# FFN 2 of a streaming-encoder layer: the third and fourth feature tile as a pair job, its operands made during the second halves of the first four units

## The chip, the cores and the metric

One core of one Trainium2 chip. The metric is the device time in microseconds of one execution of the whole layer. Times inside the layer are given on the clock of the profile, from the first instruction of the span.

## What is computed

The reference is one layer of a hybrid encoder on a sequence of 512 tokens with 1024 channels in float32. Only its last part matters here, behind the projection `w_o` of the mixed branches:

```python
h = h + rms_norm(merged @ w_o[l], mix_post_g[l])
f = swiglu(rms_norm(h, ffn2_pre_g[l]), ffn2_w1[l], ffn2_w3[l], ffn2_w2[l])
h = h + 0.5 * rms_norm(f, ffn2_post_g[l])
# swiglu(x, w1, w3, w2) = (silu(x @ w1) * (x @ w3)) @ w2, hidden width D_FF = 2816
```

The first FFN, the input projection, the recurrent branch and the attention come before it and are not touched.

## The kernel before

Every matrix product is made of three products of split operands: a float32 tile is split into a high part (ACT's copy to a shorter format) and a low part (DVE's difference), and the PE adds high x high, low x high and high x low into one PSUM bank. `split2` is one such split: one ACT and one DVE instruction. Weights of an FFN come as feature tiles of 128 columns ("w1b 0" is the first of W1 of FFN 2, "w3b 0" of W3); there are 22 of each.

FFN 2 makes the hidden features in two ways. A *classic unit* takes one feature tile: 8 slices of k times 3 products of 128x512 (`mm_feat`, L201 to L203). A *pair job* takes two feature tiles of the same matrix and the four quarters of x^T (two halves of the channels by two halves of the tokens), and makes the 2x2 block product with seven block products instead of eight (`Pairs.run`); each block product is `mm_s`: 4 slices of k times 3 products of 128x256 (L452 to L454). For that, sums of weight blocks are wanted (`S12`, `S34`, made by `prep(m, 0)` with four additions, on POOL unless told otherwise, L497 to L500, and split by `prep(m, 2)` and `prep(m, 3)`), the first weight tile split (`prep(m, 1)`) and the last block (`prep(m, 4)`), and sums of the quarters of x^T (`sums`: the tiles T, from the four unsplit quarters `xf`; split by `to_slots` and `to_uT` into t1 to t4). In `run`, the first product goes into the bank `bu` and ACT copies it to q1 (L529); the second goes into `bx` and is copied to q5; the third adds on to `bu`. Job m belongs to W1 (even m) or W3 (odd m).

Every engine runs its instructions in the order in which the program issues them. Work that is to run beside later products is put off by `later(n, ...)` and issued at the n-th following `point()`; the queues of loads are SP's, `order` gives the loads' order, and `dma_to`, `split_to` and `get` issue loads and splits up to a given place of it. All large tiles share 42 slots of 4 KB for each partition; a tile takes its slot at its first write, and slots are handed out in the order in which they were freed. A load therefore waits on SP until the last reader of the slot's former tile is done.

`tok_gemm` makes a product with tokens as rows (here merged @ W_o) in four row tiles, with a norm after each (`norms`: L264, L276 and others on DVE, L275 and L283 on ACT), and then transposes the normed rows to x^T (`transpose_mm` on PE, `transpose_out` and `transpose_xf` on ACT and DVE; uT holds x^T split, `xf` unsplit). While the last row tiles are normed, the PE makes the *first halves* (tokens 0 to 255) of the first four classic units, w1b 0, w3b 0, w1b 1, w3b 1; the last transposes stand ahead of the fourth of these. The *second halves* (tokens 256 to 511) follow, then the function returns. Before the change four more classic units come then (w1b 2, w3b 2, w1b 3, w3b 3, NC2 = 4), and the sums of x^T, their splits and the operands of job 0 are issued by `later` during these; then 18 pair jobs.

Of the kernel before, what the change touches and what calls it, by code (L numbers as in the profile page):

```python
# [13 lines left out]
ALU = mybir.AluOpType  # L14
# [4 lines left out]
KT = D // P  # L19
# [32 lines left out]
def hybrid_layer(ctx: ExitStack, tc: tile.TileContext, a: dict, out: bass.AP):  # L52
    nc = tc.nc
    act, dve, pool, pe, sp = nc.scalar, nc.vector, nc.gpsimd, nc.tensor, nc.sync
# [120 lines left out]
    def later(n, fn, rank=1):  # L175
        uid[0] += 1
        due.append((now[0] + n, rank, uid[0], fn))
# [128 lines left out]
    def transpose_xf(banks, t, xf):  # L306
        for half, ps in enumerate(banks):
            v = ps.rearrange("p (k c) -> p k c", k=4)
            act.activation(xf[half, t // 2][:, :, (t % 2) * P : (t % 2 + 1) * P], v, AF.Copy)


    def tok_gemm(nm, xs, n, R, gpost_name, scale, gpre_name, first, x_to=None, xf=None, spill=False):

        F = n - R
        acc = {}
        w = {}

        def accs(t):  # L320
            if t not in acc:
                acc[t] = [bank("acc"), bank("acc")]
            return acc[t]

        pre = min(2, F)
        x_to = x_to or (lambda k: None)
        for k in range(pre):
            x_to(k + 1)
            w[k] = get(nm, k, ahead=pre - k + 1)
        if pre:  # L330
            for tt in ((0, 1), (2, 3)):
                for k in range(pre):
                    for t in tt:
                        mm_tok(accs(t), xs[k], t, w[k], k == 0, False)
                        if t % 2:
                            point()
        for k in range(pre, F):
            x_to(k + 2)
            w[k] = get(nm, k, ahead=2 + (R - 2) * (k + 1) // F)
            for t in range(NT):  # L340
                mm_tok(accs(t), xs[k], t, w[k], k == 0, False)
                if t % 2:
                    point()
        point(True)
        for k in range(F, n):
            x_to(k + 1)
            w[k] = get(nm, k, ahead=max(0, n - 1 - k), rawahead=2)
        gpost = bcast(gpost_name)
        gpre = bcast(gpre_name) if gpre_name else None
        us, trs = {}, {}  # L350
        split_to(st["get"] + len(first))
        dma_to(st["split"] + 2)
        for t in range(NT):
            for ns in ((0,), (1,)):
                for k in range(F, n):
                    mm_tok(accs(t), xs[k], t, w[k], k == 0, k == n - 1, ns)
            if not gpre_name:
                o = slot([P, D], name="o")

                def store(nn, c, t=t, o=o):  # L360
                    sp.dma_start(out=out[t * P : (t + 1) * P, c], in_=o[:, c])

                post_norm(acc[t], t, gpost, scale, o, store)
                continue
            if t == NT - 1:
                break
            if t >= 1:
                trs[t - 1] = transpose_mm(us[t - 1])
            if t == NT - 2:

                transpose_out(trs[t - 1], t - 1)
            us[t] = norms(acc[t], t, gpost, scale, gpre, spill)
            if t == NT - 2 and xf:
                transpose_xf(trs[t - 1], t - 1, xf)
            elif t == 1:
                transpose_out(trs[t - 1], t - 1, xf)
        if not gpre_name:
            return
        t = NT - 1
        ws, bs = [], []  # L380
        for i, key in enumerate(first):
            ws.append(get(*key, ahead=len(first) - 1 - i, rawahead=2))
            bs.append(bank("f"))
            if i == len(first) - 1:
                trs[t] = transpose_mm(us[t])
                transpose_out(trs[t], t)
                if xf:
                    transpose_xf(trs[t - 1], t - 1, xf)
                    transpose_xf(trs[t], t, xf)
            mm_feat(bs[i], ws[i], 0, 256)  # L390
            if i == 0:
                trs[t - 1] = transpose_mm(us[t - 1])
                us[t] = norms(acc[t], t, gpost, scale, gpre, spill)
                transpose_out(trs[t - 1], t - 1)
        get_ahead()
        for w_, b in zip(ws, bs):
            mm_feat(b, w_, 256, 512)
        return bs
# [58 lines left out]
    class Pairs:  # L457
# [13 lines left out]
        def prep(self, m, i, eng=None):  # L471
            if m >= len(self.jobs) or (m, i) in self.ready:
                return
            self.ready.add((m, i))
            k = self.k0 + 2 * m
            if i == 0:
                if k not in loaded or k + 1 not in loaded:
                    self.raws(m)
                s12, s34 = slot([P, 2 * QH], name="S12"), slot([P, 2 * QH], name="S34")
                self.w[m] = {"r": (raws.pop(k), raws.pop(k + 1)), "s": (s12, s34)}  # L480
            W = self.w[m]
            (ra, rb), (s12, s34) = W["r"], W["s"]
            a11, a12, a21, a22 = ra[:, :QH], ra[:, QH:], rb[:, :QH], rb[:, QH:]

            def both(src, w=2 * QH):
                hi = slot([P, w], F32R, name="whi")
                lo = slot([P, w], F32R, name="wlo")
                split2(hi, lo, src)
                return hi, lo

            def halves(p, a, b):
                W[a] = p[0][:, :QH], p[1][:, :QH]
                W[b] = p[0][:, QH:], p[1][:, QH:]

            if i == 0:
                e = eng or pool
                e.tensor_tensor(out=s12[:, :QH], in0=a21, in1=a22, op=ALU.add)  # L497
                e.tensor_tensor(out=s12[:, QH:], in0=s12[:, :QH], in1=a11, op=ALU.subtract)
                e.tensor_tensor(out=s34[:, QH:], in0=a12, in1=s12[:, QH:], op=ALU.subtract)
                e.tensor_tensor(out=s34[:, :QH], in0=a11, in1=a21, op=ALU.subtract)  # L500
            elif i == 1:
                halves(both(ra), "a11", "a12")
            elif i == 2:
                halves(both(s12), "s1", "s2")
            elif i == 3:
                halves(both(s34), "s3", "s4")
            elif i == 4:
                t = slot([P, 2, QH], F32R, name="w22")
                split2(t[:, 0, :], t[:, 1, :], a22)
                W["a22"] = t[:, 0, :], t[:, 1, :]  # L510
                del W["r"], W["s"]
# [109 lines left out]
    hid, X1 = Hidden(), {}  # L621
# [96 lines left out]
    def uview(hh, th):  # L718

        return lambda e, k: uT[:, e, 4 * hh + k, th * 256 : th * 256 + 256]  # L720
# [1 line left out]
    def pair_view(p):  # L722
        return lambda e, k: p[e][:, k, :]

    def sums(xf):

        t = [slot([P, 4, 256], name="T") for _ in range(4)]
        pool.tensor_tensor(out=t[2], in0=xf[1, 1], in1=xf[0, 1], op=ALU.subtract)
        dve.tensor_tensor(out=t[0], in0=xf[0, 1], in1=xf[0, 0], op=ALU.subtract)
        dve.tensor_tensor(out=t[1], in0=xf[1, 1], in1=t[0], op=ALU.subtract)  # L730
        dve.tensor_tensor(out=t[3], in0=xf[1, 0], in1=t[1], op=ALU.subtract)
        return t
# [21 lines left out]
    for k in range(KT):  # L754
        later(2 + k // 2, lambda k=k: norm_x(k))
    later(6, lambda: xts.clear())
    later(6, lambda: tn.extend(sums(xn)))
    later(7, lambda: X1.update(b11=to_slots(xn[0, 0])))
    later(9, lambda: X1.update(t1=to_slots(tn[0])))
    later(11, lambda: X1.update(t2=to_slots(tn[1])))  # L760
# [342 lines left out]
    mg = []  # L1103
# [16 lines left out]
    del xh, xl, OH, OL, KS, QS, BT  # L1120
    h_load([h_scr[t] for t in range(NT)])
    xf = {(hh, th): slot([P, 4, 256], name="xf") for hh in range(2) for th in range(2)}
    bs = tok_gemm("wo", mg, KT, RO, "mix_post_g", 1.0, "ffn2_pre_g", [("w1b", 0), ("w3b", 0), ("w1b", 1), ("w3b", 1)], xf=xf)


    hid = Hidden()
    X2, tn = {"b11": uview(0, 0), "b21": uview(1, 0), "b22": uview(1, 1)}, []
    later(1, lambda: hid.f.append(silu_mul(bs[0], bs[1])))
    later(2, lambda: hid.f.append(silu_mul(bs[2], bs[3])))
    later(1, lambda: tn.extend(sums(xf)))  # L1130
    later(2, lambda: xf.clear())
    for i in range(3):
        later(2 + i, lambda i=i: X2.update({f"t{i + 1}": to_slots(tn[i])}))
    pairs_b = Pairs("w1b", "w3b", NC2, X2, hid)
    end = 2 * 2 * (NC2 - 2)
    for i, at_ in enumerate((end - 7, end - 4, end - 3, end - 2, end - 1)):
        later(at_, lambda i=i: pairs_b.prep(0, i))
    later(end, lambda: pairs_b.prep(1, 0))
    swiglu_units("w1b", "w3b", 2, NC2, hid)
    point(True)  # L1140
    X2["t4"] = to_uT(tn[3], 0, 1)
    tn.clear()
    pairs_b.run(w2_ahead)
    X2 = pairs_b = None
    tok_gemm("w2b", hid, FT, RF, "ffn2_post_g", 0.5, None, [], hid.to)
# [13 lines left out]
RO = 6  # L1159

NC1 = 6
NC2 = 4


# [52 lines left out]
```

## Time and profile before

| | |
|---|---|
| median of 3 runs | 1138.76 us (1138.6 to 1138.85) |
| the profiled execution, its own time | 1138.66 us |
| its span, first to last instruction | 1136.9 us |
| PE, DVE, ACT, POOL busy | 1128.2, 778.7, 582.2, 340.7 us |
| first halves begin on PE | 781.94 us |
| second halves begin | 795.44 us |
| classic units of tiles 2 and 3 begin | 806.96 us |
| pair jobs begin | 828.75 us |

A row of the order of time reads: start, duration, engine, line, operation, what is written and read, shapes (and how many were merged); in brackets the idle time of the engine before it and what ended it. Matmuls overlap in the pipeline: the distance between their starts is what one costs, not the duration shown. A row of waits reads: who, for what, us in total, times, longest.

### The profile page before, as it was taken

To read this page: it belongs to the slowest core of one execution; us is meant where nothing else is said; L and a number is where in the kernel's file an instruction comes from. 1 tells how busy PE (TensorE), PEld (TensorE's weight loads), DVE (VectorE), ACT (ScalarE), POOL (GpSimd) and SP (SyncE) were. 2 spreads that over 40 slices of the span, in tenths; PEclk is the share of its full clock that TensorE was granted. 3 is DMA by queue.
4 is the path that set the end of the run, shared out by engine and by line. 5 is a ranking of instruction groups with operands and counts; after the bars stand their busy time and mean duration, and the time that the engine had idled before them with its cause. 6 is when DMAs were issued, how large, how long until landed. Compare 5 with 4: busy or idle time off the path is not lost.

```text
span 1136.9 us, 17091 instructions
## 1 busy us (share of the span) xinstructions
PE 1128.2 (99%) x6691; PEld 1001.0 (88%) x6691; DVE 778.7 (68%) x1183; ACT 582.2 (51%) x1036; POOL 340.7 (30%) x257
## 2 busy tenths in 40 slices
PE   9999999999999999999999999999999999999997
PEld 7889999988889977888888888889899999998886
DVE  5997889885436745684778854667968678985313
ACT  7445555564325369944656652356445555574211
POOL 0148677500001000001555640000655567700000
PEclk9999999999999999999999999999999999999999
DMA  9943223264314311334122333532123332254101
GB/s 343 158 132 112 96 92 111 82 216 157 104 55 146 132 56 56 90 96 130 56 85 83 93 109 98 176 118 93 39 93 112 112 103 84 93 193 176 40 19 55
DMA packets 36800, 124.93 MB, mean 110 GB/s; under 512 B 4400, under 2 KB 5936, under 8 KB 36720
## 3 DMA queue, kind: packets, MB, share of 16 engines
q1 hardware_dynamic: 34128, 115.15, 30.3%
q0 software_dynamic: 2448, 8.43, 3.8%
q8 instruction: 52, 0.85, 0.3%
q10 hardware_dynamic: 144, 0.26, 0.1%
q14 instruction: 28, 0.23, 0.1%
HBM read 116.50 MB, written 7.33 MB: 109 GB/s over the span
## 4 chain that ended last, share of the span: by engine, by line
PE 97%; DVE 2%; ACT 0%; issue 0%; DVEq 0%
PE f L201 11%; PE f L202 11%; PE f L203 11%; PE c L454 10%; PE c L453 10%; PE c L452 10%; PE acc L220 8%; PE acc L221 8%; PE acc L219 8%; PE pt L1032 1%; PE s L996 1%; PE s L995 1%; PE tr L292 1%; PE r L832 1%; PE o L1048 1%; PE o L1049 1%
## 5 line engine op out<-in xcount | busy, mean ns | idle before, releaser
L201 PE MATMUL f<-uT,whi 128*128 128x512 f32 (+1 forms) x536 | 197.1, 368 | 0.0
L202 PE MATMUL f<-uT,wlo 128*128 128x512 f32 (+1 forms) x536 | 195.3, 364 | 0.3 <-DVE wlo L157 0.3
L203 PE MATMUL f<-uT,whi 128*128 128x512 f32 (+1 forms) x536 | 195.0, 364 | 0.0
L219 PE MATMUL acc<-whi,hT 128*128 128x512 f32 x352 | 137.1, 390 | 0.0
L220 PE MATMUL acc<-wlo,hT 128*128 128x512 f32 x352 | 137.0, 389 | 0.0
L221 PE MATMUL acc<-whi,hT 128*128 128x512 f32 x352 | 136.9, 389 | 0.0
L201 PEld LDWEIGHTS f<-uT,whi 128*128 128x128 f32 x536 | 101.1, 189 | 18.4 <-issue 2.9
L192 DVE TENSOR_TENSOR wlo<-S,whi 128x1024 fp32r<-128x1024 f32 x68 | 112.9, 1660 | 4.0 <-ACT whi L191 3.7
L453 PE MATMUL c<-Xh,wlo 128*128 128x256 f32 x408 | 115.5, 283 | 0.0
L454 PE MATMUL c<-Xl,whi 128*128 128x256 f32 x408 | 115.5, 283 | 0.0
L453 PE MATMUL c<-uT,wlo 128*128 128x256 f32 x408 | 115.5, 283 | 0.0
L454 PE MATMUL c<-uT,whi 128*128 128x256 f32 x408 | 115.5, 283 | 0.0
L452 PE MATMUL c<-Xh,whi 128*128 128x256 f32 x408 | 115.5, 283 | 0.0
L452 PE MATMUL c<-uT,whi 128*128 128x256 f32 x408 | 115.5, 283 | 0.0
L202 PEld LDWEIGHTS f<-uT,wlo 128*128 128x128 f32 x536 | 101.2, 189 | 16.1 <-DVE wlo L157 0.7
L203 PEld LDWEIGHTS f<-uT,whi 128*128 128x128 f32 x536 | 101.1, 189 | 16.1
L1016 POOL TENSOR_SCALAR P<-P,d 128x256 f32<-128x256 f32 (+1 forms) x64 | 63.8, 1011 | 55.5 <-DVE d L1014 33.2
L452 PEld LDWEIGHTS c<-Xh,whi 128*128 128x128 f32 x408 | 78.3, 192 | 0.0
L452 PEld LDWEIGHTS c<-uT,whi 128*128 128x128 f32 x408 | 78.3, 192 | 0.0
L453 PEld LDWEIGHTS c<-uT,wlo 128*128 128x128 f32 x408 | 78.3, 192 | 0.0
L453 PEld LDWEIGHTS c<-Xh,wlo 128*128 128x128 f32 x408 | 78.3, 192 | 0.0
L454 PEld LDWEIGHTS c<-Xl,whi 128*128 128x128 f32 x408 | 78.3, 192 | 0.0
(309 smaller groups left out, 2684.5 us busy)
## 6 DMA issues: line engine op xcount, KB each, us to landing
raw_w2a<-in_w2a_dram SPq DMA_DIRECT2D x22, 512.0 KB, 3.7
raw_w1b<-in_w1b_dram SPq DMA_DIRECT2D x22, 512.0 KB, 4.0
raw_w3b<-in_w3b_dram SPq DMA_DIRECT2D x22, 512.0 KB, 3.9
raw_w2b<-in_w2b_dram SPq DMA_DIRECT2D x22, 512.0 KB, 4.2
raw_w3a<-in_w3a_dram SPq DMA_DIRECT2D x21, 512.0 KB, 4.4
raw_w1a<-in_w1a_dram SPq DMA_DIRECT2D x20, 512.0 KB, 4.4
raw_wg<-in_wg_dram SPq DMA_DIRECT2D x16, 512.0 KB, 3.8
raw_xr<-in_xr_dram SPq DMA_DIRECT2D x8, 512.0 KB, 4.1
```

Source lines behind the costliest of these rows:

```text
L192: dve.tensor_tensor(out=lo, in0=src, in1=f32(hi), op=ALU.subtract)
L201: pe.matmul(ps[:, c0:c1], wh[:, s], h_, start=k == 0, stop=False)
L202: pe.matmul(ps[:, c0:c1], wl[:, s], h_, start=False, stop=False)
L203: pe.matmul(ps[:, c0:c1], wh[:, s], l_, start=False, stop=k == KT - 1)
L219: pe.matmul(acc[n], x[:, 0, c], wh[:, s], start=first, stop=False)
L220: pe.matmul(acc[n], x[:, 0, c], wl[:, s], start=False, stop=False)
L221: pe.matmul(acc[n], x[:, 1, c], wh[:, s], start=False, stop=last)
L292: pe.transpose(ps[:, k * P : (k + 1) * P], hg[:, kk * P : (kk + 1) * P], ident)
L452: pe.matmul(ps, wh[:, s], xh, start=first, stop=False, skip_group_check=True)
L453: pe.matmul(ps, wl[:, s], xh, start=False, stop=False, skip_group_check=True)
L454: pe.matmul(ps, wh[:, s], xl, start=False, stop=k == 3, skip_group_check=True)
L1016: pool.tensor_scalar(out=pt[:, x, b0:256], in0=pt[:, x, b0:256], scalar1=d[:, x : x + 1], scalar2=None, op0=ALU.mult)
```

## The change

NC2 goes from 4 to 2: feature tiles 2 and 3 of W1 and W3 become pair jobs 0 and 1 (20 jobs instead of 18). `tok_gemm` gets a hook `then`, called behind the last transposes' copies and ahead of the products of the fourth unit's first half. In the hook are issued: the four subtractions of `sums` (all on DVE; one was POOL's), the split of job 0's first weight tile, the splits t1 and t2, the S12 and S34 additions of job 0 (on DVE), and the split of S12. After `tok_gemm`, in this order: the silu and product of the first feature tile, the load and the POOL additions for job 1, t3, the split of S34, the silu and product of the second tile, the split of the last block of job 0, the split of job 1's first weight tile, and t4. `prep` allows step 1 to come before step 0.

```diff
@@ -309,7 +309,7 @@
             act.activation(xf[half, t // 2][:, :, (t % 2) * P : (t % 2 + 1) * P], v, AF.Copy)
 
 
-    def tok_gemm(nm, xs, n, R, gpost_name, scale, gpre_name, first, x_to=None, xf=None, spill=False):
+    def tok_gemm(nm, xs, n, R, gpost_name, scale, gpre_name, first, x_to=None, xf=None, spill=False, then=lambda: None):
 
 
 
@@ -387,6 +387,7 @@
                 if xf:
                     transpose_xf(trs[t - 1], t - 1, xf)
                     transpose_xf(trs[t], t, xf)
+                then()
             mm_feat(bs[i], ws[i], 0, 256)
             if i == 0:
                 trs[t - 1] = transpose_mm(us[t - 1])
@@ -473,7 +474,7 @@
                 return
             self.ready.add((m, i))
             k = self.k0 + 2 * m
-            if i == 0:
+            if m not in self.w:
                 if k not in loaded or k + 1 not in loaded:
                     self.raws(m)
                 s12, s34 = slot([P, 2 * QH], name="S12"), slot([P, 2 * QH], name="S34")
@@ -722,10 +723,10 @@
     def pair_view(p):
         return lambda e, k: p[e][:, k, :]
 
-    def sums(xf):
+    def sums(xf, eng):
 
         t = [slot([P, 4, 256], name="T") for _ in range(4)]
-        pool.tensor_tensor(out=t[2], in0=xf[1, 1], in1=xf[0, 1], op=ALU.subtract)
+        eng.tensor_tensor(out=t[2], in0=xf[1, 1], in1=xf[0, 1], op=ALU.subtract)
         dve.tensor_tensor(out=t[0], in0=xf[0, 1], in1=xf[0, 0], op=ALU.subtract)
         dve.tensor_tensor(out=t[1], in0=xf[1, 1], in1=t[0], op=ALU.subtract)
         dve.tensor_tensor(out=t[3], in0=xf[1, 0], in1=t[1], op=ALU.subtract)
@@ -754,7 +755,7 @@
     for k in range(KT):
         later(2 + k // 2, lambda k=k: norm_x(k))
     later(6, lambda: xts.clear())
-    later(6, lambda: tn.extend(sums(xn)))
+    later(6, lambda: tn.extend(sums(xn, pool)))
     later(7, lambda: X1.update(b11=to_slots(xn[0, 0])))
     later(9, lambda: X1.update(t1=to_slots(tn[0])))
     later(11, lambda: X1.update(t2=to_slots(tn[1])))
@@ -1120,26 +1121,33 @@
     del xh, xl, OH, OL, KS, QS, BT
     h_load([h_scr[t] for t in range(NT)])
     xf = {(hh, th): slot([P, 4, 256], name="xf") for hh in range(2) for th in range(2)}
-    bs = tok_gemm("wo", mg, KT, RO, "mix_post_g", 1.0, "ffn2_pre_g", [("w1b", 0), ("w3b", 0), ("w1b", 1), ("w3b", 1)], xf=xf)
-
-
-    hid = Hidden()
-    X2, tn = {"b11": uview(0, 0), "b21": uview(1, 0), "b22": uview(1, 1)}, []
-    later(1, lambda: hid.f.append(silu_mul(bs[0], bs[1])))
-    later(2, lambda: hid.f.append(silu_mul(bs[2], bs[3])))
-    later(1, lambda: tn.extend(sums(xf)))
-    later(2, lambda: xf.clear())
-    for i in range(3):
-        later(2 + i, lambda i=i: X2.update({f"t{i + 1}": to_slots(tn[i])}))
+
+    hid, tn = Hidden(), []
+    X2 = {"b11": uview(0, 0), "b21": uview(1, 0), "b22": uview(1, 1)}
     pairs_b = Pairs("w1b", "w3b", NC2, X2, hid)
-    end = 2 * 2 * (NC2 - 2)
-    for i, at_ in enumerate((end - 7, end - 4, end - 3, end - 2, end - 1)):
-        later(at_, lambda i=i: pairs_b.prep(0, i))
-    later(end, lambda: pairs_b.prep(1, 0))
-    swiglu_units("w1b", "w3b", 2, NC2, hid)
-    point(True)
+
+    def operands():
+        tn.extend(sums(xf, dve))
+        pairs_b.prep(0, 1)
+        X2["t1"] = to_slots(tn[0])
+        X2["t2"] = to_slots(tn[1])
+        pairs_b.prep(0, 0, dve)
+        pairs_b.prep(0, 2)
+
+    bs = tok_gemm("wo", mg, KT, RO, "mix_post_g", 1.0, "ffn2_pre_g", [("w1b", 0), ("w3b", 0), ("w1b", 1), ("w3b", 1)], xf=xf, then=operands)
+
+
+    xf.clear()
+    hid.f.append(silu_mul(bs[0], bs[1]))
+    pairs_b.prep(1, 0)
+    X2["t3"] = to_slots(tn[2])
+    pairs_b.prep(0, 3)
+    hid.f.append(silu_mul(bs[2], bs[3]))
+    pairs_b.prep(0, 4)
+    pairs_b.prep(1, 1)
     X2["t4"] = to_uT(tn[3], 0, 1)
     tn.clear()
+    del bs
     pairs_b.run(w2_ahead)
     X2 = pairs_b = None
     tok_gemm("w2b", hid, FT, RF, "ffn2_post_g", 0.5, None, [], hid.to)
@@ -1159,7 +1167,7 @@
 RO = 6
 
 NC1 = 6
-NC2 = 4
+NC2 = 2
 
 
 # ---- launch: one core; inputs laid out for contiguous loads ----
```

## The prediction

> **What bounds the kernel now.** I read the page first, then the PE's waits, then the order of time around the stretch that the change rewrites (776 to 850 us) on PE, DVE, ACT, POOL and SP.
>
> ```profile
> span 1136.9 us, 17091 instructions
> PE 1128.2 (99%) x6691; PEld 1001.0 (88%) x6691; DVE 778.7 (68%) x1183; ACT 582.2 (51%) x1036; POOL 340.7 (30%) x257
> PE 97%; DVE 2%; ACT 0%; issue 0%; DVEq 0%
> ```
>
> ```profile
> PE w L603 <- DVE tiny L608: 1.5, 1, 1.5
> PE f L202 <- DVE wlo L157: 0.3, 1, 0.3
> ```
>
> The PE is busy for 99% of the span, the chain that ended last is 97% PE, and the whole run holds two PE waits worth naming, 1.8 us together. So a product that disappears is time gained, and a wait put before a product is time lost, one for one. The order of time on PE gives the prices of the stretch:
>
> ```profile
> 791.19 0.28 PE L202 MATMUL f<-uT,wlo 128*128 128x256 f32 x1
> 791.31 0.28 PE L203 MATMUL f<-uT,whi 128*128 128x256 f32 x1
> 791.67 1.06 PE L292 MATMUL tr<-ident,hg 128*128 128x128 f32 x8
> ...
> 795.44 0.28 PE L201 MATMUL f<-uT,whi 128*128 128x256 f32 x1
> ...
> 806.96 0.40 PE L201 MATMUL f<-uT,whi 128*128 128x512 f32 x1
> ...
> 828.75 0.28 PE L452 MATMUL c<-uT,whi 128*128 128x256 f32 x1
> ...
> 838.82 0.28 PE L452 MATMUL c<-Xh,whi 128*128 128x256 f32 x1
> ...
> 848.90 0.28 PE L452 MATMUL c<-Xh,whi 128*128 128x256 f32 x1
> ```
>
> The second halves of the first four units run from 795.44 to 806.96, the four classic units of tiles 2 and 3 to 828.75, then the pair jobs. The same product of consecutive jobs starts 10.08 us apart (838.82 to 848.90), so one of a job's seven products takes 1.44 us. Ahead of the last transposes stands an edge: the last two products before them start at 791.19 and 791.31, 0.12 apart, and they come at 791.67. They already wait 0.24 us for the normed row tile, so whatever makes that later delays the PE in full.
>
> **Part 1, the products.** Four classic units go: 828.75 - 806.96 = 21.79 us. Two pair jobs come: 2 x 10.08 = 20.16. Gain 1.63 us. The splits, silus and sums of the removed units on ACT and DVE are replaced by a pair's; that matters only where the PE waits for them, next.
>
> **Part 2, POOL's sums for job 1 are moved ahead.** Before, POOL's first work of this stretch waited for xf; the change takes that subtraction off POOL and gives it the four sums of job 1 as its first work. Its queue is then empty, so they start when their weights (w3b 2 and 3) land.
>
> ```profile
> 779.86 0.33 SPq L141 DMA_DIRECT2D raw_w1b<-in_w1b_dram  x1
> 780.28 0.38 SPq L141 DMA_DIRECT2D raw_w3b<-in_w3b_dram  x1
> 781.48 0.39 PE L220 MATMUL acc<-wlo,mg 128*128 128x512 f32 x1
> 781.71 0.39 PE L221 MATMUL acc<-whi,mg 128*128 128x512 f32 x1
> DMA to landing us min/median/max: 3.6/3.9/4.6
> ```
>
> Loads take slots in the order in which these were freed. Before, the next load got a slot that a W_o product had left at 779.86. After, the tiles that the new function writes stand ahead in line: four T, two for the first weight, four for t1 and t2, S12, S34, two for S12's split: 14. Before, four split tiles stood there. Ten places further are the slots of the very last products, which start at 781.48 and 781.71 and last 0.39. So w3b 2 is loaded at about 781.9, w3b 3 at 782.3 (0.42 later, as 779.86 and 780.28 are). The second of two loads in a row I put near the upper end of 3.6 to 4.6: landed at 786.8, POOL starts at 786.9 (786.0 to 787.0). There DVE is in the middle of the last row tile's norm:
>
> ```profile
> 786.71 0.75 DVE L264 SCALAR_TENSOR_TENSOR h<-fg,r,h 128x512 f32<-128x512 f32 x1
> 787.57 0.69 DVE L276 TENSOR_TENSOR hg<-h,bc_ffn_pre_g 128x512 f32<-128x512 f32 x1
> 788.18 0.75 DVE L264 SCALAR_TENSOR_TENSOR h<-fg,r,h 128x512 f32<-128x512 f32 x1
> 788.96 0.69 DVE L276 TENSOR_TENSOR hg<-h,bc_ffn_pre_g 128x512 f32<-128x512 f32 x1
> ```
>
> What a POOL sum does to such an operation is seen later in the same trace:
>
> ```profile
> 837.63 1.30 POOL L497 TENSOR_TENSOR S<-raw_w3b 128x512 f32<-128x512 f32 x1 [4.54 <-PE c L454]
> 838.00 1.21 DVE L557 TENSOR_TENSOR cc<-ct 128x256 f32<-128x256 f32 x1 [0.30 <-ACT ct L556]
> 839.13 1.78 DVE L192 TENSOR_TENSOR w<-raw_w3b,w 128x512 fp32r<-128x512 f32 x1
> 848.25 0.42 DVE L557 TENSOR_TENSOR cc<-ct 128x256 f32<-128x256 f32 x1
> 822.91 0.68 DVE L192 TENSOR_TENSOR w<-raw_w1b,w 128x512 fp32r<-128x512 f32 x1
> ```
>
> L557 takes 0.42 alone and 1.21 beside POOL's sum: it ends at 839.21, so its own 0.42 began at 838.79, just before the sum's end at 838.93. A 512 split goes from 0.68 to 1.78 likewise. The two take turns, each waiting for the other's whole instruction, with a hand-over 0.13 us before the recorded end. Played through: L264 786.71 to 787.46, POOL 787.3 to 788.6, L276 788.5 to 789.2, POOL 789.05 to 790.35, L264 790.2 to 790.95, POOL 790.8 to 792.1, L276 792.0 to 792.7. In the trace of before that last one ends at 789.65: 3.0 us late. The fourth sum lies against the small operations of the root; I add 0.2 and take 3.2. The norm, the transposes and the PE slip by it.
>
> The ends: if POOL is 0.2 us earlier and gets ahead of the first L264, one more turn fits, 4.1. No row shows a scalar_tensor_tensor beside a POOL sum; if only L276 takes turns (0.4 each), 0.8. I take 3.2 because L264 reads two SBUF tiles as L276 and L557 do. The Trainium skill ("SBUF — State Buffer", Who interferes with whom) says that a VectorE instruction with two SBUF inputs and a GpSimd one that reads SBUF exclude each other for the whole instruction. The tensor_tensor rows above agree, no row here shows L264; by it L264 waits too and the term is 3.2, by the rows of tensor_tensor alone 0.8, which would make the sum 2.4 us smaller.
>
> **Part 3, job 0's operands.** Everything that used to be spread over 22 us of classic units is now queued behind the last transposes' copies:
>
> ```profile
> 792.27 2.48 DVE L302 TENSOR_TENSOR uT<-tr,uT 128x512 fp32r<-128x512 f32 x4 [0.75 <-ACT uT L301]
> 808.22 1.23 DVE L731 TENSOR_TENSOR T<-xf,T 128x1024 f32<-128x1024 f32 x1
> 820.04 1.21 DVE L192 TENSOR_TENSOR wlo<-S,whi 128x1024 fp32r<-128x1024 f32 x1
> 793.57 2.08 ACT L309 ACTIVATE xf<-tr 128x512 f32<-128x512 f32 x4
> 798.51 1.28 ACT L409 ACT_TABLE_LOAD   x1
> 799.80 0.60 ACT L409 ACTIVATE sw<-f 128x512 f32<-128x512 f32 x1
> 808.28 2.01 ACT L191 ACTIVATE Xh<-T 128x1024 fp32r<-128x1024 f32 x2 [0.30 <-DVE T L730]
> 814.08 0.62 ACT L191 ACTIVATE w<-raw_w1b 128x512 fp32r<-128x512 f32 x1
> 830.38 0.38 ACT L529 ACTIVATE ct<-c 128x256 f32<-128x256 f32 x1 [3.32 <-PE c L454]
> ```
>
> On the clock of before (part 2 shifts all of it together, PE included): xf is complete at 795.65. DVE then makes four sums of 1024 and three low parts (first weight, t1, t2), 7 x 1.2 = 8.4, then two S12 additions of 512, 2 x 0.7: S12 is there at 805.5. POOL is done by then. ACT has been waiting for S12 and in its own order has still ahead of it: split of S12 1.0, table load 1.28, silu 0.6, t3 1.0, S34 1.0, silu 0.5, a22 0.6, job 1's first weight 1.0, t4 1.0: 8.0 us, less 0.3 for overlapped starts. So the copy q1 of the first product begins at 813.2 and ends at 813.6. The PE starts job 0 at 806.96, needs S12's low part at 808.4 (ACT's part at 806.5, then 1.2 on DVE: 807.7, no wait) and, 2 x 1.44 later, at 809.85, its third product, which adds onto the bank that q1 reads, and so must wait for q1. Wait: 813.6 - 809.85 = 3.7 us. Queued behind it are the other products alone; S34 (wanted four products in), t3 and t4 are ready in time.
>
> Ends: 2.4, if each ACT item is 0.15 cheaper, and 4.6, if POOL still takes turns with the sums. The loads for job 2 take slots that the second halves free near 801; their POOL sums, from about 806, would meet the S34 and t3 splits and cost DVE some 1.1 us each, but those are wanted only after q1. The cover is q1's wait; without it they would cost the PE about 1 us.
>
> **Sum.** -1.63 + 3.2 + 3.7 = +5.3 us. The profiled execution took 1138.66 us (span 1136.9 and 1.76 around it), 0.1 under the median of the runs. 1138.66 + 5.3 = 1144.0 us.
>
> **Rivals.**
>
> *Load late or no turn-taking on the norm.* If w3b 3 lands only after 791, or the norm's operations are not held up, part 2 falls to 0 to 0.8: 1140.7 to 1141.5 us. For it: L264 has no row beside a POOL sum. Against: 4.6 is the longest landing of these loads.
>
> *The operands are hidden, as the change says* (the other side). Its mechanism is ACT's lead on the PE: q1 must begin right behind the first product. The wait is worth less than the products' gain only if q1 ends before 811.5, that is if ACT's list is 2.1 us shorter than read, and the norm isn't held up. Fully covered: 1138.66 - 1.63 = 1137.0 us. For it: ACT is busy only half the time in this trace, and no PE wait of the sort exists before. Against: ACT's order is fixed, and it can't begin S12's split before DVE's nine operations.
>
> *The clock drops after the waits.* Each wait leaves the PE idle for over 3 us, and no row of before shows an idle PE of that length. If it then ran at half pace for as long as it stood (24 products of 256 in 5.8 instead of 2.9 us), it would lose half of 3.4 and half of 3.7, 3.5 us: 1147.5. The Trainium skill ("TensorE: Matmul & The Clock Gate", Part 1) puts the clock at half "after ≥1 idle window (~3.4µs)", free-running, so that idle times of just this length seldom hold a whole window. Nothing here shows it.
>
> **How the numbers follow.** Both waits: 0.68, 1144.0 us, own range 1142.2 to 1145.6. Norm not held up: 0.16, about 1141. Clock drop: 0.07, 1147.5. Hidden: 0.09, about 1137, of which a little lands within the change. A measurement of this kernel tells about 0.2%, 2.3 us, from no change: 1141.1 and up is slower, so half of the second rival counts as the same. Faster by that much, below 1136.5, needs a gain greater than the products': 0.03. Same: 0.15. Slower: 0.82. The range reaches from the second rival to the bound of both terms at their upper ends (4.1 and 4.6 make 1145.7) with part of a clock drop: 1140.4 to 1146.5; it leaves out hidden and most of the clock drop.
>
> **What would show it.** Part 1: 96 products of 128x512 fewer (32 on each of three lines), two pair jobs more, their spacing still 10.08. Part 2: POOL's L497 at about 787, L264 and L276 of the last row tile at 1.8 instead of 0.7, the transposes near 794.9. Part 3: a PE wait of some 3.7 us on ACT's ct, line of q1, inside the first job. Wrong would be: POOL's first sum after 792, or q1 ending within 0.5 us of the first product.

## The result, and the profile after

| | before | after |
|---|---|---|
| median | 1138.8 us (1138.6 to 1138.87) | 1144.78 us (1144.13 to 1145.88) |
| ratio to before | | 1.0054, 95% interval 1.0041 to 1.0067 |
| the profiled execution: time, span | 1138.66, 1136.9 us | 1145.83, 1143.9 us |

The kernel became 6.0 us slower; 1144.0 was predicted. In the code after, the lines behind `tok_gemm`'s hook have numbers one higher (q1 is copied on L530, a pair job's products are L453 to L455). The page of after: span, busy times, the chain that ended last by engine, and the first line of a classic unit's products:

```profile
span 1143.9 us, 17267 instructions
PE 1128.6 (99%) x6763; PEld 1004.5 (88%) x6763; DVE 794.1 (69%) x1199; ACT 587.3 (51%) x1049; POOL 340.4 (30%) x260
PE 91%; DVE 5%; ACT 2%; issue 1%; DMA 0%; SPq 0%; DVEq 0%; ACTq 0%
L201 PE MATMUL f<-uT,whi 128*128 128x512 f32 (+1 forms) x504 | 184.8, 367 | 0.0
```

L201 stood at x536 before: 32 products fewer on each of three lines, 96 in all, as the change says. The PE's busy time did not fall, and the waits of the PE (who, for whom, us in total, times, longest) hold two rows that were not there:

```profile
PE c L453 <- ACT ct L530: 3.4, 1, 3.4
PE tr L292 <- DVE hg L282: 3.2, 1, 3.2
```

Both in the order of time of the PE:

```profile
791.71 0.28 PE L203 MATMUL f<-uT,whi 128*128 128x256 f32 x1
795.16 1.06 PE L292 MATMUL tr<-ident,hg 128*128 128x128 f32 x8 [3.17 <-DVE hg L282]
...
813.22 0.28 PE L455 MATMUL c<-Xl,whi 128*128 128x256 f32 x1
816.91 0.39 PE L453 MATMUL c<-Xh,whi 128*128 128x256 f32 x1 [3.41 <-ACT ct L530]
...
818.85 0.42 PE L455 MATMUL c<-Xl,whi 128*128 128x256 f32 x1
819.06 0.41 PE L453 MATMUL c<-uT,whi 128*128 128x256 f32 x1
...
825.68 0.28 PE L453 MATMUL c<-Xh,whi 128*128 128x256 f32 x1
```

The last transposes start 3.45 us behind the product ahead of them, 0.36 before: 3.09 lost. The third product of job 0 starts 3.69 behind the second, 0.12 without a wait: 3.57 lost. Behind it the same products come 0.21 apart instead of 0.12. Stretches of that time, with the granted clock in the third column from the end:

```profile
817.00:818.00 1.00, 1.00 (x8) 1.00 (x9) 1.00 (x2) 0.13 (x1) 0.92 (x2) 0.82 0.00 0
818.00:821.00 3.00, 3.00 (x16) 3.00 (x16) 3.00 (x2) 1.70 (x3) 3.00 (x2) 0.50 0.00 0
821.00:825.00 4.00, 4.00 (x35) 4.00 (x35) 4.00 (x5) 1.13 (x3) 1.62 (x3) 0.99 0.00 0
```

The clock is at half for 3.4 us (817.6 to 821.0; such a stretch is called a drop below). What that costs is read from the starts: the 60 products from 816.91 to 825.68 take 8.77 us, where 60 x 0.12 make 7.20. So 1.57 us are lost, 0.10 of them in the first step behind the wait and about 1.5 in the slow stretch. The account of this execution: +0.40 that stands already ahead of the stretch (the product in front of the transposes starts at 791.71, at 791.31 before), -1.63, +3.09, +3.57, +1.57 make +7.00, and the spans differ by 1143.9 - 1136.9 = 7.0. The time differs by 1145.83 - 1138.66 = 7.17; the other 0.17 lies outside the span. The +0.40 is scatter between executions and not the change: in the kept traces of all kernels the first halves begin anywhere from 781.47 to 782.34.

The cause of the first wait, DVE and then POOL around the last norm:

```profile
787.12 0.75 DVE L264 SCALAR_TENSOR_TENSOR h<-fg,r,h 128x512 f32<-128x512 f32 x1
787.98 1.60 DVE L276 TENSOR_TENSOR hg<-h,bc_ffn_pre_g 128x512 f32<-128x512 f32 x1
789.50 1.78 DVE L264 SCALAR_TENSOR_TENSOR h<-fg,r,h 128x512 f32<-128x512 f32 x1
791.31 1.66 DVE L276 TENSOR_TENSOR hg<-h,bc_ffn_pre_g 128x512 f32<-128x512 f32 x1
793.57 0.54 DVE L237 SCALAR_TENSOR_TENSOR e<-r,v 128x1 f32<-128x1 f32 x1
```

```profile
787.48 1.55 POOL L498 TENSOR_TENSOR S<-raw_w3b 128x512 f32<-128x512 f32 x1 [48.81 <-DMA raw_w3b<-in_w3b_dram]
789.11 1.62 POOL L499 TENSOR_TENSOR S<-S,raw_w3b 128x512 f32<-128x512 f32 x1
```

Against 0.69, 0.75, 0.69 and 0.22 alone, the four held-up operations lose 0.91 + 1.03 + 0.97 + 0.32 = 3.23 us. And the cause of the second wait, ACT's order:

```profile
808.82 1.06 ACT L191 ACTIVATE whi<-S 128x1024 fp32r<-128x1024 f32 x1 [4.93 <-DVE S L499]
...
816.47 0.38 ACT L530 ACTIVATE ct<-c 128x256 f32<-128x256 f32 x1
```

ACT waits 4.93 us for DVE's S12 and then works 7.65 us through its list until q1's turn comes.

### The profile page after: what moved, and what is told of

It is laid out like the page before. It is cut to its first block, busy times and chain, and to the rows that moved or that the text cites. A ratio compares the mean times of both kernels' runs of the same rounds, so it can differ in the third digit from the quotient of the medians.

```text
span 1143.9 us, 17267 instructions
## 1 busy us (share of the span) xinstructions
PE 1128.6 (99%) x6763; PEld 1004.5 (88%) x6763; DVE 794.1 (69%) x1199; ACT 587.3 (51%) x1049; POOL 340.4 (30%) x260
## 4 chain that ended last, share of the span: by engine, by line
PE 91%; DVE 5%; ACT 2%; issue 1%; DMA 0%; SPq 0%; DVEq 0%; ACTq 0%
PE c L453 11%; PE c L455 11%; PE c L454 11%; PE f L201 10%; PE f L202 10%; PE f L203 10%; PE acc L221 8%; PE acc L219 8%; PE acc L220 8%; PE pt L1033 1%; PE s L997 1%; PE s L996 1%; PE r L833 1%; DVE h L264 1%; PE o L1049 1%
## 5 line engine op out<-in xcount | busy, mean ns | idle before, releaser
L201 PE MATMUL f<-uT,whi 128*128 128x512 f32 (+1 forms) x504 | 184.8, 367 | 0.0
L202 PE MATMUL f<-uT,wlo 128*128 128x512 f32 (+1 forms) x504 | 183.0, 363 | 0.3 <-DVE wlo L157 0.3
L203 PE MATMUL f<-uT,whi 128*128 128x512 f32 (+1 forms) x504 | 182.8, 363 | 0.0
L453 PE MATMUL c<-Xh,whi 128*128 128x256 f32 x432 | 122.7, 284 | 3.4 <-ACT ct L530 3.4
L453 PE MATMUL c<-uT,whi 128*128 128x256 f32 x432 | 122.8, 284 | 0.0
L455 PE MATMUL c<-uT,whi 128*128 128x256 f32 x432 | 122.8, 284 | 0.0
L454 PE MATMUL c<-uT,wlo 128*128 128x256 f32 x432 | 122.8, 284 | 0.0
L455 PE MATMUL c<-Xl,whi 128*128 128x256 f32 x432 | 122.8, 284 | 0.0
L454 PE MATMUL c<-Xh,wlo 128*128 128x256 f32 x432 | 122.6, 284 | 0.0
L201 PEld LDWEIGHTS f<-uT,whi 128*128 128x128 f32 x504 | 95.2, 189 | 17.2 <-issue 2.9
L203 PEld LDWEIGHTS f<-uT,whi 128*128 128x128 f32 x504 | 95.2, 189 | 14.8
L202 PEld LDWEIGHTS f<-uT,wlo 128*128 128x128 f32 x504 | 95.2, 189 | 14.7 <-DVE wlo L157 0.7
L453 PEld LDWEIGHTS c<-Xh,whi 128*128 128x128 f32 x432 | 83.2, 193 | 3.7 <-ACT ct L530 3.6
L453 PEld LDWEIGHTS c<-uT,whi 128*128 128x128 f32 x432 | 83.6, 193 | 0.0
L455 PEld LDWEIGHTS c<-uT,whi 128*128 128x128 f32 x432 | 83.4, 193 | 0.0
L455 PEld LDWEIGHTS c<-Xl,whi 128*128 128x128 f32 x432 | 83.3, 193 | 0.0
```

The source lines that it names most:

```text
L201: pe.matmul(ps[:, c0:c1], wh[:, s], h_, start=k == 0, stop=False)
L202: pe.matmul(ps[:, c0:c1], wl[:, s], h_, start=False, stop=False)
L203: pe.matmul(ps[:, c0:c1], wh[:, s], l_, start=False, stop=k == KT - 1)
L453: pe.matmul(ps, wh[:, s], xh, start=first, stop=False, skip_group_check=True)
L454: pe.matmul(ps, wl[:, s], xh, start=False, stop=False, skip_group_check=True)
L455: pe.matmul(ps, wh[:, s], xl, start=False, stop=k == 3, skip_group_check=True)
```

## The experiments

The code cuts are shortened: `...` stands for lines left out, and words in square brackets for the calls that do what they name. In the kernels with `hooks`, a key (n, i) names work that is issued behind the copy of job n's i-th product (1: q1, 2: q5, 3: u); `run` of after has that argument and gives it nothing.

**POOL's instructions with one input.** Is the first wait a matter of two instructions that both read two tiles?

```diff
-    pairs_b.prep(1, 0)
+    pairs_b.prep(1, 0, one_input)   # pool.tensor_scalar(out, in0, vec[:, 0:1], mult) for each addition
```

This kernel leaves out the second operand of each addition.

> POOL's four operations for job 1 keep their place, size and operands' order but read one tile each (a product with a column of constants in place of the addition), so the operands of the first W3 pair are left out and its features are not those of the layer. Theory A (POOL and DVE take turns only where both read two SBUF tiles): L264 and L276 of the last row tile fall back from 1.6-1.8 to 0.75 and 0.69 us, the PE wait for hg before the last transposes goes from 3.2 to about 0.2 us, the wait for q1 stays at 3.4, time about 3 us under the changed kernel (1144.8 to about 1141.5). Theory B (any POOL operation that reads SBUF holds up DVE operations with two SBUF inputs): the four rows stay at 1.5 us or more, the wait for hg at 2 us or more, time within 1 us of the changed kernel. Rival C (the transposes wait for something else, such as the load traffic at 786): the wait stays though L264 and L276 are short.

Measured 1143.04 us, ratio 1.0038 (1.0025 to 1.0052). DVE and POOL of that kernel:

```profile
787.70 0.99 DVE L276 TENSOR_TENSOR hg<-h,bc_ffn_pre_g 128x512 f32<-128x512 f32 x1
788.62 0.74 DVE L264 SCALAR_TENSOR_TENSOR h<-fg,r,h 128x512 f32<-128x512 f32 x1
789.39 1.07 DVE L276 TENSOR_TENSOR hg<-h,bc_ffn_pre_g 128x512 f32<-128x512 f32 x1
```

```profile
787.12 1.92 POOL L1132 TENSOR_SCALAR S<-raw_w3b,vec 128x512 f32<-128x512 f32 x1 [48.73 <-DMA raw_w3b<-in_w3b_dram]
789.12 1.67 POOL L1132 TENSOR_SCALAR S<-S,vec 128x512 f32<-128x512 f32 x1
```

POOL works in the same place, but L264 runs beside it at its own 0.74, and L276 loses 0.30 to 0.38 instead of 0.91 to 0.97. The PE's wait at the transposes falls from 3.2 to 1.1. So POOL's presence slows DVE a little, and two thirds of the wait go when POOL's instruction reads one tile instead of two. The kernel changes the operation with it (tensor_scalar for tensor_tensor); which of the two matters is not separated. The measured value lies between the two theories: neither none nor all of it.

**ACT's order ahead of q1.** Only the splits of S12, S34 and the last block stay ahead of q1; t3, t4, both silus and the split of job 1's first weight are issued between the products.

```diff
-    hid.f.append(silu_mul(bs[0], bs[1]))
     pairs_b.prep(1, 0)
-    X2["t3"] = to_slots(tn[2])
...
+    hooks = {(0, 1): [t3], (0, 2): [t4], (0, 3): [silu of tile 0], (1, 1): [silu of tile 1]}
+    pairs_b.run(w2_ahead, hooks)
```

> Same work; ACT's list ahead of q1 is cut: t3, t4, both silus and job 1's first weight are issued behind q1, q5 and u inside the first job; only the splits of S12, S34 and the last block stay ahead. POOL's clash with the norm stays. Theory (the PE's third product waits for q1 and nothing else, because ACT's list is too long): the wait for q1 goes from 3.4 to under 0.3 us, no clock drop follows it, the hg wait stays 3.2: time about 1140.7 if nothing takes the wait's place, up to 1142.7 if DVE, which now has no slack, makes job 1's S12 split late (a PE wait of up to 2 us on wlo). Rival (the third product waits for DVE's S12 low part or for t2): the wait stays near 3 us under another name.

Measured 1142.81 us, 1.0037 (1.0024 to 1.005). The PE's waits:

```profile
PE tr L292 <- DVE hg L282: 3.1, 1, 3.1
PE w L604 <- DVE tiny L609: 1.4, 1, 1.4
PE c L454 <- DVE wlo L192: 0.5, 1, 0.5
```

The wait at q1 is gone with ACT's order alone changed. A wait of 0.5 on a low half took its place, and the half clock (795.2, for 3.4 us) now stands behind the first wait, whose length did not change. With one wait of two taken away the kernel gained 2.0 us, not 3.4: 0.5 is the new wait, and a drop behind the first wait, which the wait at q1 would have swallowed (as the next two kernels show), now costs its full price, 1.5: from the transposes at 794.68 to job 0's first product at 811.50 it is 16.82 us, where the changed kernel, with full clock there, takes 15.30.

**One split behind q1, and one copy more ahead of it.** These two change the size of the second wait alone: t4's split (0.95 us on ACT) goes behind q1, or a copy of 1024 elements is put in front of it.

```diff
-    X2["t4"] = to_uT(tn[3], 0, 1)
-    tn.clear()
...
-    pairs_b.run(w2_ahead)
+    pairs_b.run(w2_ahead, {(0, 1): [lambda: X2.update(t4=to_uT(tn[3], 0, 1)), tn.clear]})
```

> One ACT item of 0.95 us (the split t4) is moved from ahead of q1 to behind it; nothing else. Theory (q1's place in ACT's list sets the wait; an idle PE of more than about 3.4 us sometimes halves the clock for 3.4 us and costs 1.7): wait 2.5 us, no stretch of clock 0.50 in the profile, all runs within 0.5 us of each other, median about 1143.3, that is 0.95 under the lower group of the changed kernel's runs (1144.1 to 1144.5) and 2.5 under the upper (1145.1 to 1145.9). Rival (the clock drop comes from something else, as the load burst or the total of both waits): runs still in two groups 1.5 us apart.

```diff
+    idle = slot([P, D], name="idle")
+    act.activation(idle, h[0], AF.Copy)
     pairs_b.run(w2_ahead)
```

> One ACT copy of 1024 (0.95 us, its result unused) is added ahead of q1. Theory: wait 4.4 us, clock at 0.50 for some 3.4 us behind it in the profile, more runs in the upper group or all of them: median about 1146.5 to 1147 (1144.3 + 0.95 + 1.7), spread under that of the changed kernel if all drop. Rival (the drop is rare and unrelated to this wait): median 1145.3 to 1145.7 with the same two groups. Against both: under 0.5 us more, if q1 isn't what the PE waits for.

Measured 1143.59 us, 1.0043 (1.003 to 1.0055), and 1146.46 us, 1.0066 (1.0054 to 1.0079). The waits of the first, then of the second:

```profile
PE tr L292 <- DVE hg L282: 3.1, 1, 3.1
...
PE c L453 <- ACT ct L530: 1.0, 1, 1.0
```

```profile
PE tr L292 <- DVE hg L282: 3.1, 1, 3.1
PE c L453 <- ACT ct L530: 2.9, 1, 2.9
```

3.4 - 0.95 would be 2.5, and 3.4 + 1 would be 4.4. The traces show 1.0 and 2.9, about 1.5 less in both. In both of these profiled executions the clock fell behind the first wait (from 794.8 and 795.3, 3.4 us): the PE then comes 1.5 later to q1's wait and waits that much less. For the first kernel no stretch at half clock had been expected. So the two waits are not independent: a drop behind the first costs nothing as long as the second outlasts it. In the profiled execution of after it fell behind the second and cost about 1.5. By account, the second kernel without a drop that costs is 1144.5 and with one 1146.0; its five runs are 1144.7 (the profiled one) and 1145.99 to 1146.8. Between the two profiled executions, whose clock fell at the same place, the lists differ by some 1.9 us, the waits by 1.9 and the times by 1.74 (1142.96 and 1144.7): what ACT does ahead of q1 passes on to the time nearly one for one. That the clock makes the rest of the spread is not shown, since the other runs have no trace.

**POOL taken out of the stretch.** Job 1's additions on DVE behind the splits:

```diff
-    pairs_b.prep(1, 0)
+    pairs_b.prep(1, 0, dve)
```

> Job 1's four additions are made by DVE at the same place of the program, POOL has no work beside the last norm. Theory (POOL's additions hold up the norm): L264 and L276 of the last row tile at 0.75 and 0.69 us, PE wait for hg from 3.2 to 0.2-0.3, q1's wait unchanged at 3.4 with or without a clock drop behind it. DVE gets 2.6 us more ahead of t3, S34 and job 1's operands and loses its slack, so a new PE wait of 0 to 2 us on wlo or w. Time 1141 to 1143, against 1144.8 of the changed kernel. Rival (the transposes wait for the load traffic or for ACT): the hg wait stays near 3.

Measured 1142.96 us, 1.0038 (1.0024 to 1.0052).

```profile
PE c L453 <- ACT ct L530: 3.4, 1, 3.4
```

No wait at the transposes is left: it was POOL. The wait at q1 keeps its 3.4, so the two have separate causes. The medians gain 1.8 here, less than 3.1: in the profiled execution the clock stood at half from 811.8 for 6.8 us, two stretches of 3.4, of which 5.5 were work of the PE. At 0.21 instead of 0.12 for a product that is 2.4 us lost, against about 1.5 in the trace of after.

**The one subtraction back on POOL.** With T2 on POOL, as it was before the change, POOL has work that waits for xf ahead of job 1's additions, and these no longer reach the norm.

```diff
-        tn.extend(sums(xf, dve))
+        tn.extend(sums(xf, pool))
```

> One part undone: the subtraction t2 stays on POOL as before the change, ahead of job 1's additions, which so wait for xf. Theory (POOL's and DVE's two-tile operations take turns wherever they meet, so the clash moves and does not vanish): hg wait 0.2-0.3, but t2 (2.3 us) and the four additions (1.1 each) now hold up the chain that makes S12: less t2's own 1.1 on DVE, S12 some 5 us later, q1's wait from 3.4 to 8-9 us with a clock drop in every run: time 1146.5 to 1149. Rival (the norm's slip alone was the harm of the move): hg wait gone and q1's wait about 1 us shorter: 1140.5 to 1141.5.

Measured 1147.34 us, 1.0077 (1.0063 to 1.009).

```profile
PE c L453 <- ACT ct L530: 2.9, 1, 2.9
PE c L453 <- ACT whi L191: 2.6, 1, 2.6
...
PE c L454 <- DVE wlo L192: 0.9, 1, 0.9
```

The clash moved from the norm into the sums of x^T and came back as two waits on operands, 3.5 us together, beside a wait at q1 of 2.9, with the clock at half for 10.2 us from 811.0. Five POOL operations beside a DVE that is on the way to the PE cost their turns here too; the worst kernel of the study is the one that only moved them.

**Both cures together, first form.** ACT's order nearly as above (t3 stays ahead of q1), and job 1's additions get a slot that is only freed by the last norm's L276, so POOL starts behind the wide operations.

```diff
+    pairs_b.raws(1)
     pairs_b.prep(0, 3)
     pairs_b.prep(0, 4)
+    X2["t3"] = to_slots(tn[2])
+    pairs_b.prep(1, 0)
+    hooks = {(0, 2): [t4], (0, 3): [silu of tile 0], (1, 1): [silu of tile 1]}
```

> Both waits attacked, same work. The loads for job 1 are issued where they were, but POOL's additions are issued behind the splits of S34, the last block and t3, so that their result takes the slots of the last norm's gain and square: they start when L276 has ended, at about 790, and end before the sums begin. ACT has only the splits of S12, S34, the last block and t3 ahead of q1; the rest comes inside jobs 0 and 1. Theory: hg wait 0.3 to 0.8 (only the root's small operations meet POOL), no q1 wait, no clock drop; DVE still meets POOL's additions for job 2 and may be up to 1.7 us late with job 1's splits: 1137.3 to 1139.3, the whole gain of 1.63 left in the best case. Rival (a late split takes the waits' place whatever is done): 1140 or more.

Measured 1140.92 us, 1.0018 (1.0009 to 1.0026). DVE's norm of that kernel:

```profile
789.92 0.65 DVE L237 SCALAR_TENSOR_TENSOR e<-r,v 128x1 f32<-128x1 f32 x1
790.60 0.15 DVE L242 TENSOR_SCALAR e<-e 128x1 f32<-128x1 f32 x1
790.79 1.13 DVE L243 TENSOR_TENSOR r<-r,e 128x1 f32<-128x1 f32 x1
791.95 1.57 DVE L282 TENSOR_SCALAR hg<-hg,r 128x512 f32<-128x512 f32 x1
```

POOL starts at 789.26 as meant, but meets the root's small operations: L243, one element for each partition, goes from 0.16 to 1.13, L237 from 0.22 to 0.65, L282 from 0.48 to 1.57. The transposes still come late (a PE wait of 2.6) and the clock still falls. The runs lie in two groups, 1139.49 to 1140.11 and 1140.92 to 1141.66, about 1.5 apart by their means, with mean clocks of 0.998 to 0.999 and 0.996 to 0.997: without the drop and with it.

**Job 2's additions later too.**

```diff
+        (1, 2): [lambda: pairs_b.prep(2, 0), lambda: pairs_b.raws(3)],
```

> As the kernel before this one, and the loads and additions for job 2 are issued one and a half jobs later (behind job 1's second copy), so that POOL meets fewer of DVE's splits for job 1. Theory: job 1's splits on time, 1137.0 to 1138.0; new risk: job 2's S12 late by up to 2 us. Rival: the loads' slots, not their place in the program, set POOL's start, and nothing changes against the kernel before this one (within 0.3 us).

Measured 1141.46 us, 1.0025 (1.0015 to 1.0036): no gain. The edit moves less than it seems to. POOL's additions for job 2 start at 814.52 instead of 812.56 and still meet DVE's splits for job 1, and the PE waits 0.4 for job 1's S12 low half where it waited 0.2.

**POOL behind the transposes.** Job 0's weight sums are made ahead of the sums of x^T, and job 1's additions take the slot of the last hg, which the transposes free. In the first of two kernels a one-column POOL operation holds job 2's additions back until job 1's split is done; the second is without it.

```diff
     def operands():
+        pairs_b.prep(0, 0, dve)
+        pairs_b.prep(0, 1)
+        pairs_b.prep(0, 2)
         tn.extend(sums(xf, dve))
...
+        pool.tensor_tensor(out=gate, in0=lo[:, :1], in1=lo[:, 1:2], op=ALU.add)   # the first kernel only
+        pairs_b.prep(2, 0)
```

> Same work, other order. The additions and splits of S12 and of job 0's first weight, which don't need x^T, are issued ahead of the sums of x^T; ACT then has only t1, t2, S34, the last block, t3 and both silus between the sums and q1; POOL's additions for job 1 take the slot that the last normed row tile leaves when it is transposed, so they start at about 792.5, behind the whole norm; POOL's additions for job 2 are held behind job 1's S12 split by a one-column addition that reads it. Theory: no PE wait above 0.3 us between 780 and 850, no clock drop, so the gain of the products alone is left: 1138.6 - 1.6 = 1137.0, range 1136.7 to 1137.8. Rival 1: DVE as a whole has too little time between 795 and 817 (some 20 of 22 us), a PE wait of 1 to 2 us on a low part stays: 1138 to 1139.5. Rival 2: job 2's S12 comes late: the same size, at job 2.

> As the kernel before this one without the one-column addition: POOL's additions for job 2 start when their loads land, at about 809. Theory (each POOL addition beside DVE's splits costs these 1.1 us): job 1's S12 split up to 4 us later on DVE, of which 0.5 to 3 show as a PE wait on wlo in job 1: 1137.5 to 1140. Rival (DVE has slack there): the same as the kernel before this one within 0.3 us.

Measured 1142.55 us, 1.003 (1.0019 to 1.0041), and 1141.19 us, 1.0019 (1.001 to 1.0028). The second kernel's waits and DVE's sums:

```profile
PE c L453 <- ACT ct L530: 2.3, 1, 2.3
```

```profile
799.94 2.32 DVE L730 TENSOR_TENSOR T<-xf,xf 128x1024 f32<-128x1024 f32 x1
802.18 2.31 DVE L731 TENSOR_TENSOR T<-xf,xf 128x1024 f32<-128x1024 f32 x1
```

No wait at the transposes is left in either. Two of POOL's additions now hold up two sums of x^T (2.3 us against 1.2), and with the table load and the silus ahead of it on ACT q1 is late again, by 2.3. Holding job 2's additions back made it worse: those of the later jobs come late with them, and the PE waits 0.3 and 0.5 us for two low halves of job 3 (at 840.5 and 842.7). Without the drop (1139.61 and 1139.79) the second kernel is within 1.1 us of before; by their times and mean clocks (0.996 to 0.998) nine of its runs have it.

**ACT's list ahead of q1 cut, on top of that.** First the silus (2.26 us with their table load) go behind q5 and later, and one split of job 1's weights (1.04) comes ahead of q1 in their place; then t3, that split and job 0's last split go behind q1 too.

```diff
-    hid.f.append(silu_mul(bs[0], bs[1]))
-    hid.f.append(silu_mul(bs[2], bs[3]))
+    pairs_b.prep(1, 1)
     pairs_b.prep(1, 0)
...
+        (0, 3): [silu of tile 0], (1, 1): [silu of tile 1], (1, 2): [job 2's additions],
```

> The kernel of the early first operands (1141.19, or about 1139.7 where the clock stayed up) with ScalarE's work ahead of q1 cut: the table load and the two gatings (2.26 us from 809.28 to 811.54 there) go behind the second and the eighth product, and one split of job 1's raw weights (1.08) takes their place, so that job 1's sums keep their buffer and GpSimd still starts behind the transposes. Theory (the wait at q1 is what ScalarE does ahead of it, and the half clock follows a wait of over 2 us): the wait falls from 2.3 to 1.1, the clock stays at 1.00, and the time is 1138.9 - 1.6 for the drop taken out of the usual runs, that is 1138.0 to 1138.9, level with the kernel before. Rival (VectorE, busy without a gap from 794 to 817 there, is as late as ScalarE): the wait only changes its name to one on a low half on VectorE, the drop stays, 1140 to 1141.5.

```diff
     pairs_b.prep(0, 3)
-    pairs_b.prep(0, 4)
-    X2["t3"] = to_slots(tn[2])
-    pairs_b.prep(1, 1)
-    pairs_b.prep(1, 0)
+    hooks = {(0, 1): [t3, job 1's split, job 1's additions, job 0's last split],
```

> As the run before, and the fourth operand pair of the input, the split of job 1's raw weights and job 0's last split go behind q1 on ScalarE too: ahead of it stands only what the first products need. Theory: q1 is written as soon as its product ends, no wait of TensorE on it and none at the transposes, no half clock; the twelve products that the pairs save are left whole: 1136.9 to 1137.6, 0.1% below the kernel before. Rival (VectorE is as late): a wait of 0.5 to 2 us on a low half in job 0 or 1 appears in its place, 1138 to 1140.

Measured 1139.32 us (1139.01 to 1140.01), 1.0006 (0.9997 to 1.0015), and 1139.53 us (1139.03 to 1141.01), 1.001 (1.0001 to 1.0019). Waits of the first and of the second:

```profile
PE c L453 <- ACT ct L530: 0.9, 1, 0.9
PE c L454 <- DVE wlo L192: 0.8, 1, 0.8
```

```profile
PE c L454 <- DVE wlo L192: 1.9, 1, 1.9
```

The first theory had the wait and the clock right and the time 0.4 us too low; for the second its rival came true. The wait at q1 falls as ACT's list does, 2.3, 0.9, nothing, and no clock drop is in the first kernel's trace. But DVE has been busy without a gap since the transposes, and the low half of job 1's S12 comes late: the PE now waits for DVE 8 us later. The rows show that POOL's additions for job 2 meet DVE once more on this way. In the first of these kernels they start at 811.99, and three of DVE's splits, the last of them that low half, take 2.31, 2.32 and 1.72 us:

```profile
812.48 2.31 DVE L192 TENSOR_TENSOR wlo<-raw_w3b,whi 128x1024 fp32r<-128x1024 f32 x1
814.71 2.32 DVE L192 TENSOR_TENSOR uT<-T,uT 128x1024 fp32r<-128x1024 f32 x1
816.95 0.68 DVE L411 TENSOR_TENSOR sw<-f,sw 128x512 f32<-128x512 f32 x1
817.55 1.72 DVE L192 TENSOR_TENSOR wlo<-S,whi 128x1024 fp32r<-128x1024 f32 x1
```

Each of the three split rows takes 1.22 in the trace of the 1141.19 kernel above, where POOL was the one that waited (an addition of 4.51 us). So 2.7 us of turns stand ahead of a wait of 0.8. No kernel was run with these turns taken out and ACT's short list kept. In the second kernel (2.7 us of turns in the same stretch) that wait is 1.9 long, and three of its eleven runs (1140.78 to 1141.01, the profiled one among them) have the half clock behind it. The first of these kernels is the best of the study. It stands level with the kernel before and not below it. Its two waits eat the 1.63 us of the saved products. By the starts they cost more than the 0.9 and 0.8 of their rows: the stretches of 10.08 us in which they lie take 11.26 and 11.15, so 2.25 us are lost. 2.25 - 1.63 = +0.62; the spans differ by 0.6 (1137.5 and 1136.9).

## Why the prediction was right

*Part 1, -1.63.* 96 products of 128x512 went and two jobs came. The gain has no row of its own, but the same product of later jobs still starts 10.08 apart (835.76 to 845.84), and the account of the spans closes with it.

*Part 2, +3.2: measured 3.09, by the mechanism and the order given.* The first of the two L264 escaped, L276, L264, L276 took turns, and the fourth sum cost the root 0.32, where 0.2 was put in. POOL started at 787.48 instead of 786.9, outside the bound of 787.0 that I gave. 0.4 of this is the offset of the whole execution, which moved DVE's norm as well, so the ranking of the operations was not touched. The choice in doubt was L264: it took 1.78 beside POOL, and the two L276 lost 0.91 and 0.97, so the term that let L276 alone lose 0.4 each, 0.8, was wrong. The Trainium skill ("SBUF — State Buffer", Who interferes with whom) has a VectorE instruction with two SBUF inputs contend with a GpSimd instruction that reads SBUF. The trace of after agrees for a scalar_tensor_tensor against POOL's two-input sums. The kernel with one input does not: POOL's instruction still reads SBUF there, yet L264 ran at 0.74 and L276 lost 0.30 and 0.38; the measurement decides. The transposes start at 795.16, where 794.9 was named.

*Part 3, +3.7: measured 3.57.* On the clock of before the split of S12 was put at 805.5 and q1's start 7.7 later; the trace has 808.82, with part 2's 3.1 and the offset of 0.4 in it 805.3, and q1 7.65 behind it.

*The step that was mis-sized is the clock.* It got a chance of 0.07 and a price of 3.5 us, a half of each wait. It fell in the profiled execution. The runs of after lie in two groups (1144.13 to 1144.47 and 1145.08 to 1145.88), but the lower group is not shown to be without a drop: its mean clocks are 0.995 to 0.997, those of the upper 0.995 to 0.998. A drop behind the first wait, swallowed at q1 as in the trace of the kernel with t4 behind q1, would fit it. Wherever one of the later kernels had a PE wait of 1.9 us or more, its profiled execution had at least one drop. Its price per drop is about 1.5: it lasts 3.4 us, or a multiple, whatever the wait was, and a product takes 0.21 us in it, not the 0.24 that a half pace would make. The one behind the first wait is paid back at the second. So +5.3 was predicted where the time of the traced execution reads +7.17 and the median +6.0. The sum without it, 1144.0, is 0.1 under the lowest run and 0.8 under the median; the range had room for part of a drop, and the median lies in that part.

The other rivals fell: the norm was held up, and the operands were not hidden. The experiments show together that both waits can be taken away, one by POOL's place and one by ACT's order, and that 0.7 to 0.9 us then still stands against the change. In the best kernel that is the rest of the wait at q1 and the wait for job 1's S12 low half, ahead of which POOL's additions for job 2 hold DVE up. The sums and splits used to lie under 22 us of classic units; whether they could be hidden without that cover, if POOL's turns were taken out as well, is open.

## What to carry to other kernels

A unit of work that is replaced because its products are more than are needed can also be the cover under which the operands of what follows are made: before it goes, play its engines' lists through to the first instruction that the PE waits for. Work put on an idle engine is not free when its instruction reads two tiles beside a busy DVE; place it by what frees its slot, and look for the DVE operation that it will meet, the one-column ones of a root too. Two waits in a row add where the first delays all engines, as the norm's did here (3.09 and 3.57); what the PE alone loses between them, as by a slow clock, is won back at the second. So curing the second wait can uncover a loss that it had covered.

## What the hardware showed that was not expected

- The clock drop needs less idle time than the wait of 3.4 us. It came behind PE waits of 3.2, 2.6, 2.3 and 1.9 us; in one kernel it began 2.1 us after the last product, with the PE still waiting (811.8, wait from 809.7 to 813.1). The length alone does not decide: behind the wait of 3.2 at the transposes of after the clock stayed at 1.00. None came in eleven runs whose longest wait in this stretch was 0.9: by their times, 1139.01 to 1140.01, and in the one trace. The Trainium skill ("TensorE: Matmul & The Clock Gate", Part 1) speaks of half speed after an idle window of about 3.4 us. The runs show it behind waits shorter than that. The drop itself lasts 3.4 us or a multiple in these traces: 3.4, 6.8 and 10.2.
- Turn-taking does not depend on the size of DVE's operation: 128x1 waits for POOL's whole 128x512 (0.16 to 1.13).
- A POOL operation with one input leaves a scalar_tensor_tensor of two inputs alone (0.74); it takes 1.67 to 1.92 us itself, where POOL's two-input sums took 1.55 to 1.71 in turns.
